# A fast product for the first FFN too: seven half products from inner block 4 on, and the modulation rows moved around it

## The chip, the core and the metric

The kernel runs on one core of one Trainium2 chip. TensorE (PE) multiplies, VectorE (DVE) and ScalarE (ACT) evaluate and prepare, GpSimd (POOL) helps, SyncE (SP) issues the loads. The metric is device microseconds of one execution. A profiled execution is one further run with the trace taken.

## The reference

Two layers of a diffusion backbone for 128 context tokens and 512 latents (640 columns), width 1024. Layer 0 mixes by pooling and short convolution, layer 1 by attention; each layer then has a SwiGLU FFN with 2816 inner columns:

```python
def modulate(x, g, shift, scale):
    return rms_norm(x, g) * (1 + scale) + shift
def swiglu(h, w_in, w_out):
    a, b = jnp.split(h @ w_in, 2, axis=-1)
    return (jax.nn.silu(a) * b) @ w_out
...
sh1, sc1, g1, sh2, sc2, g2 = ada_params(cond, w_ada[l], b_ada[l])   # silu(cond) @ w_ada[l] + b_ada[l]
x = x + g1 * mixer(modulate(x, norm_g[l, 0], sh1, sc1))
x = x + g2 * swiglu(modulate(x, norm_g[l, 1], sh2, sc2), w_ffn_in[l], w_ffn_out[l])
```

Context and latents have a condition each, so each modulation vector exists twice. All is float32.

## The kernel before

Everything is kept transposed: a tile has 128 features on the partitions and the 640 tokens in its columns, in two PSUM banks of 320. Each operand of a product is a pair, a rounded high part and the low rest (`pair`, L142 on ACT, L143 on DVE), and a product is three matmuls (high x high, high x low, low x high). `Stream` (`ws`) loads the weights in tiles of 1 MB on SP (three raw tiles), splits them into pairs, one step ahead for whole blocks and about three for half products, and `project` (matmuls L287) multiplies one output block per step; `Pipe` runs the evaluation of a block behind its matmuls. There are three PSUM tiles of two banks for products and two of one bank for small things (`ps_small`).

An FFN (`ffn`) cuts its 22 inner blocks in three groups of 8, 8 and 6. Per group the first product (`fi`) makes the blocks a and b, silu(a) * b goes as a pair into `hid`, and the second product (`fo`) adds to the residual (L500). A plain inner block costs 2 x 48 matmuls. In the layers of `FAST`, here only the second layer, the blocks from `PLAIN` = 4 on run in `fast_blocks` (L624): the block is cut in two halves of inputs, of outputs and of columns, and Winograd's seven half products take the place of eight: 7 x 12 = 84 matmuls. Their operands (`Ops.make`) are sums of halves of the normalised input, made by `operand_in` during the plain steps 1 to 4; the weights' sums are made on DVE in the raw tile (`weight`, L234 to L240) ahead of their split. The operands lie in one of the two big buffers (`bufA`, `bufB`) and two further tiles, and `hid` takes the place of the FFN's input.

The modulation vectors are rows of `w_ada` times silu of the two conditions. Most of them are computed on DVE by `AdaDve`: a row is 128 outputs, loaded as 512 KB (`rawa`), and four `tensor_tensor_reduce` (L365), for two conditions and two halves of the inputs, with the products written to a scratch tile `junk` in SBUF. `ada.run(n)` puts n rows at its place in the program, `keep_in_program_order` holds them near it; the tile framework's scheduler orders the other instructions of an engine by its own model, and on the chip every engine goes through its list in order. Of the 84 rows, 30 are done by the end of the mixer; in the first FFN one row goes with each step of `fi` and `fo` until the rest is done, which is in group 2's first product. Six raw buffers let the loads run ahead.

Of the kernel before, what the change touches and what calls it, by code (L numbers as in the profile page):

```python
# [9 lines left out]
F32 = mybir.dt.float32  # L10
F32R = mybir.dt.float32r
AF = mybir.ActivationFunctionType
# [3 lines left out]
P = 128  # L16
D = 1024
KB = D // P
# [3 lines left out]
HT = T // 2  # L22
# [7 lines left out]
WC = 256  # L30
GROUPS = ((0, 8), (8, 16), (16, 22))

FAST = (1,)
PLAIN = 4
RAW = 3
WINDOWS = (2, 4, 8, 16)
PAD = 8
UL = PAD + CTX + PAD + LAT + PAD
# [20 lines left out]
def hybrid_step(  # L59
# [22 lines left out]
    nc = tc.nc  # L82
# [16 lines left out]
    def ps_small(name):  # L99
        return psum.tile([P, 512], F32, tag="one", bufs=2, name=name)  # L100
# [45 lines left out]
    class Pipe:  # L146


        def __init__(self):
            self.due, self.now = [], 0  # L150
# [186 lines left out]
    class AdaDve:  # L337


        def __init__(self, jobs):  # L340
            self.todo = [(l, b0, n, b) for l, b0, n in jobs for b in range(n)]
            self.at, self.raw = 0, []

        def load(self):
            at = self.at + len(self.raw)
            if at < len(self.todo):
                raw = p1.tile([P, D], F32, tag="araw", bufs=6, name=f"rawa_{at}")
                nc.sync.dma_start(raw, wada[at])
                self.raw.append(raw)

        def run(self, rows, hold=True):
            for _ in range(rows):
                if self.at == len(self.todo):
                    return
                l, b0, n, b = self.todo[self.at]
                if not self.raw:
                    self.load()
                raw = self.raw.pop(0)
                self.at += 1
                if b == 0:  # L360
                    self.got = p1.tile([P, 8, 2, 2], F32, tag="got", bufs=2, name=f"got_{l}_{b0}")
                for c in range(2):
                    for q in range(2):
                        cols = slice(512 * q, 512 * q + 512)
                        op = V.tensor_tensor_reduce(  # L365
                            out=junk,
                            in0=raw[:, cols],
                            in1=silb[:, c, cols],
                            scale=1.0,
                            scalar=0.0,  # L370
                            op0=ALU.mult,
                            op1=ALU.add,
                            accum_out=self.got[:, b, c, q : q + 1],
                        )
# [289 lines left out]

            pipe.step(lambda: product(wt, p, to, fresh), after)

    def ffn(l, xin, hid, each=None, last=None, spare=None):


        def part_a(j, psa):  # L670
# [34 lines left out]
        for gi, (f0, f1) in enumerate(GROUPS):  # L705
# [12 lines left out]
                    operand_in(i - 1)  # L718

            def plain_keep(n, p):  # L720
                if held:
                    j = min(held)
                    keep(j, held.pop(j))

            if plain:
                project(f"fi{l}_{gi}", xin, KB, 2 * plain, in_done, ext=True, each=each)
# [10 lines left out]
    nc.sync.dma_start(sm, small)  # L737
    with tc.tile_pool(name="pool1", bufs=1) as p1:
        silb = p1.tile([P, 2, D], F32, tag="silb", name="silb")
        junk = p1.tile([P, 512], F32, tag="junk", name="junk")  # L740
        ada_raw = []

        def ada_load(ch):
            for q in range(4):
                raw = p1.tile([P, 2, 512], F32, tag="araw", bufs=6, name=f"raw_ada{ch}_{q}")
# [5 lines left out]
        ada = AdaDve(  # L751
            [(0, 4, 4)] + [(0, 8 * p, 8) for p in (2, 4, 3, 5)] + [(1, 8 * p, 8) for p in (1, 0, 2, 4, 3, 5)]
        )
        ada_load(2)
        nc.sync.dma_start(kc, konst)
        nc.sync.dma_start(x[:, 0:4, :], xT[:, 0:4, :])
# [8 lines left out]
        ws.load(2, cut=True)  # L765
        ada.load()
        ada.load()
        pwr = p1.tile([P, 512], F32, tag="pwr", name="pwr").rearrange("p (g c) -> p g c", g=4)
        nc.sync.dma_start(pwr, pw)
        ws.load(3)  # L770
        zero = p1.tile([P, 512], F32, tag="junk", name="zero")
        G.memset(zero, 0.0)
        zeror2 = p1.tile([P, 512], F32R, tag="zero", name="zeror")
        V.tensor_copy(zeror2, zero)
        zeror = zeror2[:, 0:P]
        G.memset(ones, 1.0 / D)
# [253 lines left out]
        assert ada.at == len(ada.todo)  # L1030


    with tc.tile_pool(name="pool2", bufs=1) as p2:
# [527 lines left out]
```

## Time and profile before

| what | us |
|---|---|
| median of 3 runs | 1395.49 (1394.67 to 1396.0) |
| the profiled execution, its own time | 1394.27 |
| its span, first to last instruction | 1392.5 |
| PE busy | 1355.6 |
| DVE busy | 1000.9 |
| ACT busy | 571.7 |

The busy share of an engine is a mean over the span; what a change in one stage is worth is read in that stage. The chain that ended last is followed back from the last instruction; a piece of it that belongs to PE is time in which nothing but PE's own work set the pace. Matmuls of the profile overlap, so their mean duration is about twice the time at which they follow one another.

### The profile page before, as it was taken

The page shows a single profiled execution, that of the slowest core. Times are in us where ns is not written, and L with a number is a line of the kernel's source. Part 1 is how long each engine was busy: PE and PEld are TensorE (multiplying, and loading weights), DVE is VectorE, ACT ScalarE, POOL GpSimd, SP SyncE. Part 2 cuts the span into 40 slices and gives each one's busy share as a digit, 9 for nine tenths or more (in the row PEclk, how much of TensorE's full clock was granted, in tenths as well). Part 3 has the DMA queues.
Part 4 walks back from the last instruction along what each step waited for, and adds up shares of the span by engine and source line. Part 5 has one row for each costly group of instructions (what it writes and reads, how often), then busy time and mean ns, then how long its engine had stood idle before and what let it go on. Part 6 is the DMA issues. An engine that isn't in the chain of part 4 may idle for free.

```text
span 1392.5 us, 22551 instructions
## 1 busy us (share of the span) xinstructions
PE 1355.6 (97%) x9139; PEld 1329.9 (96%) x9139; DVE 1000.9 (72%) x1998; ACT 571.7 (41%) x1013; POOL 69.9 (5%) x73
## 2 busy tenths in 40 slices
PE   6989999999999999999999999999999999999995
PEld 3889999999999999999999999999999999999995
DVE  4899989878777877754767677678873577536745
ACT  3433244322122221223566676557651254314543
POOL 3200000000000000000003121000000000000012
PEclk7999999999999999999999999999999999999998
DMA  9734445444434343212223111002122112311212
GB/s 365 257 120 171 177 141 176 160 143 140 164 137 166 127 169 133 100 64 72 103 75 94 47 46 39 31 31 92 61 94 88 61 62 91 121 61 61 76 46 76
DMA packets 36728, 154.50 MB, mean 111 GB/s; under 512 B 3984, under 2 KB 11152, under 8 KB 26000
## 3 DMA queue, kind: packets, MB, share of 16 engines
q1 hardware_dynamic: 36624, 153.07, 31.5%
q8 instruction: 71, 1.16, 0.3%
q14 instruction: 33, 0.27, 0.1%
HBM read 147.55 MB, written 2.88 MB: 108 GB/s over the span
## 4 chain that ended last, share of the span: by engine, by line
PE 90%; DVE 7%; issue 1%; ACT 1%; DMA 1%; SPq 0%; POOL 0%; DVEq 0%; POOLq 0%; ACTq 0%
PE fi L287 27%; PE fo L287 22%; PE fi L624 16%; PE pq L287 5%; PE pi L287 5%; PE po L287 4%; PE wb L287 2%; PE wa L287 2%; DVE junk L365 2%; PE o L1295 2%; PE s L1245 1%; PE t L1278 1%; DMA raw_ada<-wada 1%; PE fo L1430 1%; DVE x L1415 1%
## 5 line engine op out<-in xcount | busy, mean ns | idle before, releaser
L365 DVE CUSTOM_DVE_ANT_0 junk<-rawa,silb 128x512 f32<-128x512 f32 x336 | 236.6, 704 | 6.6 <-ACT silb L807 1.0
L287 PE MATMUL fi<-ah,wh_fi 128*128 128x320 f32 x832 | 191.6, 312 | 0.0
L287 PE MATMUL fi<-al,wh_fi 128*128 128x320 f32 x832 | 191.3, 311 | 0.0
L287 PE MATMUL fi<-ah,wl_fi 128*128 128x320 f32 x832 | 191.2, 311 | 0.0
L500 DVE SCALAR_TENSOR_TENSOR x<-fo,mod,x 128x128 f32<-128x128 f32 (+1 forms) x144 | 54.7, 434 | 131.2 <-PE fo L287 128.2
L287 PEld LDWEIGHTS fi<-al,wh_fi 128*128 128x128 f32 x832 | 141.0, 189 | 0.0
L287 PEld LDWEIGHTS fi<-ah,wh_fi 128*128 128x128 f32 x832 | 141.0, 190 | 0.0
L287 PEld LDWEIGHTS fi<-ah,wl_fi 128*128 128x128 f32 x832 | 140.7, 189 | 0.0
L142 ACT ACTIVATE wh_fi<-raw_fi 128x1024 fp32r<-128x1024 f32 x52 | 55.1, 1060 | 184.8 <-PE fi L287 135.9
L142 ACT ACTIVATE wh_fi_p<-raw_fi 128x512 fp32r<-128x512 f32 x126 | 77.3, 627 | 112.3 <-PE fi L624 64.9
L142 ACT ACTIVATE wh_fo<-raw_fo 128x1024 fp32r<-128x1024 f32 (+1 forms) x48 | 47.5, 990 | 180.5 <-PE fo L287 132.6
L143 DVE TENSOR_TENSOR wl_fi_p<-raw_fi,wh_fi_p 128x512 fp32r<-128x512 f32 x126 | 85.7, 689 | 48.3 <-ACT wh_fi_p L142 48.3
L624 PE MATMUL fi<-bh,wl_fi_p 128*128 128x320 f32 x288 | 88.9, 309 | 0.0
L624 PE MATMUL fi<-bh,wh_fi_p 128*128 128x320 f32 x288 | 88.9, 309 | 0.0
L624 PE MATMUL fi<-bl,wh_fi_p 128*128 128x320 f32 x288 | 88.4, 307 | 0.0
L287 PE MATMUL fo<-bh,wh_fo 128*128 128x320 f32 x352 | 80.6, 310 | 0.0
L287 PE MATMUL fo<-bh,wl_fo 128*128 128x320 f32 x352 | 80.5, 310 | 0.0
L287 PE MATMUL fo<-bl,wh_fo 128*128 128x320 f32 x352 | 80.4, 310 | 0.0
L287 PE MATMUL fo<-al,wh_fo 128*128 128x320 f32 x328 | 75.1, 310 | 0.0
L287 PE MATMUL fo<-ah,wh_fo 128*128 128x320 f32 x328 | 74.9, 309 | 0.0
L287 PE MATMUL fo<-ah,wl_fo 128*128 128x320 f32 x328 | 74.8, 309 | 0.0
L624 PE MATMUL fi<-xh,wh_fi_p 128*128 128x320 f32 x216 | 67.8, 319 | 0.1
(341 smaller groups left out, 3200.7 us busy)
## 6 DMA issues: line engine op xcount, KB each, us to landing
raw_fi<-wfi SPq DMA_DIRECT2D x44, 1024.0 KB, 4.8
rawa<-wada SPq DMA_DIRECT2D x84, 512.0 KB, 3.5
raw_fo<-wfo SPq DMA_DIRECT2D x16, 1024.0 KB, 5.0
raw_ada<-wada SPq DMA_DIRECT2D x12, 512.0 KB, 9.3
raw_in<-win SPq DMA_DIRECT2D x6, 1024.0 KB, 7.0
raw_fo<-wfo SPq DMA_DIRECT2D x8, 768.0 KB, 4.2
raw_qkv<-wqkv SPq DMA_DIRECT2D x6, 1024.0 KB, 4.8
raw_out<-wout SPq DMA_DIRECT2D x4, 1024.0 KB, 4.8
```

Source lines behind the costliest of these rows:

```text
L142: S.activation(h, src, AF.Copy)
L143: eng.tensor_tensor(out=l, in0=src, in1=h.bitcast(F32), op=ALU.subtract)
L287: PE.matmul(ps[:, h, 0 : hi - lo], w[a][:, k, cols], rhs[b][:, k0 + k, lo:hi], start=k == 0 and a == b, stop=k == kn - 1 and a == 1,)
L365: op = V.tensor_tensor_reduce(out=junk, in0=raw[:, cols], in1=silb[:, c, cols], scale=1.0, scalar=0.0, op0=ALU.mult, op1=ALU.add, accum_ou ...
L500: V.scalar_tensor_tensor(out=xs, in0=got[:, 0 : b - a], scalar=mod[l][:, gate0 + m, c : c + 1], in1=xs, op0=ALU.mult, op1=ALU.add,)
L624: PE.matmul(out, w[a][:, k, :], ops.get(OPERAND[p], b)[:, k, :], start=fresh and k == 0 and a == b, stop=k == ops.kn - 1 and a == 1, skip_ ...
L1245: PE.matmul(self.ps[:, hf, 0:HT], bufB[a][:, self.h, q0 : q0 + P], kt[b][:, self.kv, hf * HT : hf * HT + HT], start=n == 0, stop=n == 2,)
L1278: PE.transpose(flat(pt)[:, s * P : s * P + P], self.pe[:, s * P : s * P + P], ident)
L1295: PE.matmul(po[:, 0 : 2 * P], vt[a][:, self.kv, s * P : s * P + P], got[b][:, s, :], start=s == 0 and n == 0, stop=s == 4 and n == 2,)
L1415: (G if k % 3 == 1 else V).tensor_tensor(out=xs, in0=xs, in1=rstd[:, cols], op=ALU.mult)
L1430: PE.matmul(ps[m][:, h, 0 : hi - lo], w[m][a][:, k, :], bufA[b][:, k, cols], start=k == 0 and a == b, stop=k == kn - 1 and a == 1,)
```

## The change

`FAST` takes in the first layer: its inner blocks 4 to 21 run in `fast_blocks`. Its operands lie in `bufB` and two new tiles, `hid` is now `bufA`, the FFN's last product prepares the next layer's input in `bufB`, and the two names are swapped behind it. To make room, the first part's small tiles (raw rows, `junk`, `pwr`, `zero`) move to a pool that is closed after the mixer; from there on rows have two raw buffers (`bufs` 2), loaded anew from row 30 on, and `junk` is a small PSUM tile. The 46 rows of the first FFN are spread anew: one in each of the last three plain steps of group 0, one per fast block in group 0 and one per two fast blocks in groups 1 and 2 (at product 6), one and two by turns in the steps of the second product, one in each step of the last. The last eight rows (the second layer's second gate) move to the second FFN: two per fast block of group 0 (at products 1 and 6), with a new copy of silu of the conditions and scratch in PSUM.

```diff
-FAST = (1,)
+FAST = (0, 1)
+EARLY = 30
...
+        def home(self, own, rest, bufs, junk, silb):
+            self.own, self.rest, self.bufs, self.junk, self.silb = own, rest, bufs, junk, silb
...
-            if at < len(self.todo):
-                raw = p1.tile([P, D], F32, tag="araw", bufs=6, name=f"rawa_{at}")
-                nc.sync.dma_start(raw, wada[at])
+            if at < self.limit:
+                raw = self.own.tile([P, D], F32, tag="araw", bufs=self.bufs, name=f"rawa_{self.first + at}")
+                nc.sync.dma_start(raw, wada[self.first + at])
...
-                            out=junk,
+                            out=self.junk,
...
             def plain_keep(n, p):
+                if fast_each:
+                    fast_each(gi, n, p)
...
-            [(0, 4, 4)] + [(0, 8 * p, 8) for p in (2, 4, 3, 5)] + [(1, 8 * p, 8) for p in (1, 0, 2, 4, 3, 5)]
+            [(0, 4, 4)] + [(0, 8 * p, 8) for p in (2, 4, 3, 5)] + [(1, 8 * p, 8) for p in (1, 0, 2, 4, 3)]
...
+        assert ada.at == EARLY and not ada.raw
+        early.close()
+
         def last0(kn):
-            project("fo0_2", bufB, kn, KB, updater(0, 40, Norm("b0"), (bufA, 1, 0)), each=lambda i: ada.run(1))
-
-        ffn(0, bufA, bufB, each=lambda i: ada.run(1), last=last0)
+            project("fo0_2", bufA, kn, KB, updater(0, 40, Norm("b0"), (bufB, 1, 0)), each=lambda i: ada.run(1))
+
+        with tc.tile_pool(name="pool4", bufs=1) as p4:
+            ada.home(p4, p1, 2, ps_small("junk"), silb)
+            ada.limit = len(ada.todo)
+            ada.load()
+            ada.load()
+            more = tuple(p4.tile([P, 3 * 4 * HT], F32R, tag=t, name=t) for t in ("x0h", "x0l"))
+            ffn(
+                0,
+                bufA,
+                bufA,
+                each=lambda i, plain=False: ada.run(int(i >= 5) if plain else 1 + i % 2),
+                fast_each=lambda gi, n, p: ada.run(int(p == 6 and (gi == 0 or n % 2))),
+                last=last0,
+                spare=(tuple(t.rearrange("p a b -> p (a b)") for t in bufB), more),
+            )
+    bufA, bufB = bufB, bufA
...
-    ffn(1, bufA, bufA, last=last1, spare=(whole_b, more))
+    silb = p3.tile([P, 2, D], F32, tag="silb", name="silb1")
+    nc.sync.dma_start(silb, crows[None].broadcast_to((P, 2, D)))
+    S.activation(silb, silb, AF.Silu)
+    gates = AdaDve([(1, 40, 8)], 76)
+    gates.home(p3, p3, 2, ps_small("junk1"), silb)
+    ffn(
+        1,
+        bufA,
+        bufA,
+        last=last1,
+        spare=(whole_b, more),
+        fast_each=lambda gi, n, p: gates.run(int(gi == 0 and p in (1, 6))),
+    )
```

## Rows read from the trace of the kernel before

**Rows 1.** The page: busy time of each engine over the span.

```profile
PE 1355.6 (97%) x9139; PEld 1329.9 (96%) x9139; DVE 1000.9 (72%) x1998; ACT 571.7 (41%) x1013; POOL 69.9 (5%) x73
```

**Rows 2.** The chain that ended last, in order of time, over the first FFN (start us, length us, engine, tile, line, matmuls).

```profile
222.27 7.15 PE fi L287 x48
...
337.02 56.64 PE fo L287 x384
393.66 114.14 PE fi L287 x768
507.80 56.64 PE fo L287 x384
564.44 85.61 PE fi L287 x576
650.04 42.41 PE fo L287 x288
```

**Rows 3.** The same chain over the second FFN, whose inner blocks 4 to 21 already run in seven half products (the pieces between are left out).

```profile
935.80 7.14 PE fi L287 x48
...
1044.05 56.54 PE fo L287 x384
...
1201.42 56.54 PE fo L287 x384
1257.96 1.46 PE fi L624 x10
...
1333.62 32.00 PE fo L287 x216
```

**Rows 4.** Busy time by stretch over the second FFN: four plain blocks, four fast blocks, eight fast blocks (columns: stretch, length, busy PE, PEld, DVE, ACT, POOL with instructions, granted clock, DMA share, GB/s).

```profile
935.80:993.80 58.00, 58.00 (x393) 58.00 (x392) 53.65 (x88) 43.47 (x77) 0.00 (x0) 1.00 0.22 73
993.80:1044.00 50.20, 50.17 (x337) 48.98 (x337) 36.54 (x56) 26.09 (x52) 0.00 (x0) 1.00 0.26 86
...
1100.90:1201.40 100.50, 100.43 (x673) 98.11 (x673) 72.90 (x114) 51.86 (x102) 0.00 (x0) 1.00 0.24 85
```

**Rows 5.** The same view, the last 22 us of the second FFN's plain blocks.

```profile
972.00:993.80 21.80, 21.80 (x149) 21.80 (x148) 21.12 (x36) 16.23 (x30) 0.00 (x0) 1.00 0.15 50
```

**Rows 6.** The same view: the mixer's input product, the first FFN's second product of group 0, and that of group 2.

```profile
108.00:165.60 57.60, 57.60 (x389) 57.60 (x388) 56.80 (x131) 18.26 (x30) 0.33 (x6) 1.00 0.52 185
337.00:393.70 56.70, 56.70 (x387) 56.70 (x386) 41.49 (x100) 9.49 (x11) 0.00 (x0) 1.00 0.42 146
650.00:692.50 42.50, 42.50 (x291) 42.50 (x290) 29.42 (x56) 19.69 (x32) 0.00 (x0) 1.00 0.25 84
```

**Rows 7.** DVE in order of time in the first FFN's second product of group 0 (start us, us, line, operation, [idle before]): the first two of four partial sums of a modulation row, and what ends the step.

```profile
346.32 0.68 DVE L365 CUSTOM_DVE_ANT_0 junk<-rawa,silb 128x512 f32<-128x512 f32 x1
...
347.05 0.69 DVE L365 CUSTOM_DVE_ANT_0 junk<-rawa,silb 128x512 f32<-128x512 f32 x1
...
351.22 1.14 DVE L500 SCALAR_TENSOR_TENSOR x<-fo,mod,x 128x128 f32<-128x128 f32 x3 [2.01 <-PE fo L287]
```

**Rows 8.** DVE in order of time in the first FFN's second product of group 2: one step.

```profile
671.29 1.13 DVE L500 SCALAR_TENSOR_TENSOR x<-fo,mod,x 128x128 f32<-128x128 f32 x3 [1.64 <-PE fo L287]
672.34 0.34 DVE L479 SCALAR_TENSOR_TENSOR al<-x,sc,ah 128x128 fp32r<-128x128 f32 x1
672.60 0.95 DVE L143 TENSOR_TENSOR wl_fo<-raw_fo,wh_fo 128x768 fp32r<-128x768 f32 x1
673.47 0.82 DVE L422 TENSOR_TENSOR ssq_b<-ssq_b,sq_b 128x640 f32<-128x640 f32 x1
674.21 0.75 DVE L479 SCALAR_TENSOR_TENSOR al<-x,sc,ah 128x512 fp32r<-128x512 f32 x1
```

**Rows 9.** DVE in order of time at the seam from plain to fast blocks in the second FFN.

```profile
988.90 0.81 DVE L143 TENSOR_TENSOR al<-ea,ah 128x640 fp32r<-128x640 f32 x1
...
991.70 0.69 DVE L236 TENSOR_TENSOR raw_fi<-raw_fi 128x512 f32<-128x512 f32 x1
992.31 0.82 DVE L143 TENSOR_TENSOR al<-ea,ah 128x640 fp32r<-128x640 f32 x1
993.09 0.69 DVE L143 TENSOR_TENSOR wl_fi_p<-raw_fi,wh_fi_p 128x512 fp32r<-128x512 f32 x1
993.70 0.82 DVE L515 TENSOR_TENSOR eb<-fi,rstd 128x640 f32<-128x640 f32 x1
```

**Rows 10.** Groups of DVE instructions by line and shape: a difference whose second source is in PSUM (L651), in the second FFN's eight fast blocks.

```profile
L651 DVE TENSOR_TENSOR uv<-fi,uv 128x320 f32<-128x320 f32 x7 | 3.4, 488 | 1.6 <-PE fi L624 1.6
```

**Rows 11.** The same view over the first FFN's blocks of group 0: one with both sources in SBUF (L470), and a residual from PSUM (L500).

```profile
L470 DVE TENSOR_TENSOR rstd<-y_a,ssq_a 128x320 f32<-128x320 f32 x2 | 0.9, 490 | 0.0
...
L500 DVE SCALAR_TENSOR_TENSOR x<-po,mod,x 128x320 f32<-128x320 f32 x1 | 0.5, 544 | 0.0
```

**Rows 12.** ACT in order of time at the second FFN's start: a load of its function table and the instruction behind it.

```profile
949.20 1.28 ACT L673 ACT_TABLE_LOAD   x1
950.50 1.02 ACT L673 ACTIVATE ea<-ea 128x128 f32<-128x128 f32 x2
```

**Rows 13.** The start's SiLU of the conditioning rows (duration ns min/median/max).

```profile
L807 ACT ACTIVATE silb<-silb x1: 1892/1892/1892, 33.6 to 33.6; 128x2048 f32<-128x2048 f32 x1
```

**Rows 14.** Who SP's DMA queue waited for over the first FFN (us in total, times, longest us).

```profile
SPq L220 <- DVE wl_fi L143: 104.4, 22, 13.9
```

**Rows 15.** DMA issues over the same stretch (count, KB each, median us from issue to landing).

```profile
rawa<-wada SPq DMA_DIRECT2D x49, 512.0 KB, 3.4
```

More of the change, by code (lines that the diff above doesn't have):

```diff
@@ L337, in hybrid_step, with __init__ @@
     class AdaDve:
-        def __init__(self, jobs):
+        def __init__(self, jobs, first=0):
             self.todo = [(l, b0, n, b) for l, b0, n in jobs for b in range(n)]
-            self.at, self.raw = 0, []
+            self.at, self.raw, self.first = 0, [], first
+            self.limit = len(self.todo)
+        def home(self, own, rest, bufs, junk, silb):
+            self.own, self.rest, self.bufs, self.junk, self.silb = own, rest, bufs, junk, silb
         def load(self):
             at = self.at + len(self.raw)
-            if at < len(self.todo):
-                raw = p1.tile([P, D], F32, tag="araw", bufs=6, name=f"rawa_{at}")
-                nc.sync.dma_start(raw, wada[at])
+            if at < self.limit:
+                raw = self.own.tile([P, D], F32, tag="araw", bufs=self.bufs, name=f"rawa_{self.first + at}")
+                nc.sync.dma_start(raw, wada[self.first + at])
                 self.raw.append(raw)
@@ L360, in run @@
                 if b == 0:
-                    self.got = p1.tile([P, 8, 2, 2], F32, tag="got", bufs=2, name=f"got_{l}_{b0}")
+                    self.got = self.rest.tile([P, 8, 2, 2], F32, tag="got", bufs=2, name=f"got_{l}_{b0}")
                 for c in range(2):
@@ L365, in run @@
                         op = V.tensor_tensor_reduce(
-                            out=junk,
+                            out=self.junk,
                             in0=raw[:, cols],
-                            in1=silb[:, c, cols],
+                            in1=self.silb[:, c, cols],
                             scale=1.0,
@@ L665, in fast_blocks, with ffn @@
             pipe.step(lambda: product(wt, p, to, fresh), after)
-    def ffn(l, xin, hid, each=None, last=None, spare=None):
+    def ffn(l, xin, hid, each=None, last=None, spare=None, fast_each=None):
         def part_a(j, psa):
@@ L725, in ffn @@
             if plain:
-                project(f"fi{l}_{gi}", xin, KB, 2 * plain, in_done, ext=True, each=each)
+                project(f"fi{l}_{gi}", xin, KB, 2 * plain, in_done, ext=True, each=each and (lambda i: each(i, True)))
             if l in FAST:
@@ L739, in hybrid_step @@
         silb = p1.tile([P, 2, D], F32, tag="silb", name="silb")
-        junk = p1.tile([P, 512], F32, tag="junk", name="junk")
+        early = ExitStack()
+        p0 = early.enter_context(tc.tile_pool(name="pool0", bufs=1))
+        junk = p0.tile([P, 512], F32, tag="junk", name="junk")
         ada_raw = []
@@ L744, in ada_load @@
             for q in range(4):
-                raw = p1.tile([P, 2, 512], F32, tag="araw", bufs=6, name=f"raw_ada{ch}_{q}")
+                raw = p0.tile([P, 2, 512], F32, tag="araw", bufs=6, name=f"raw_ada{ch}_{q}")
                 nc.sync.dma_start(raw, wada0[(ch + 1) // 2 if ch < 3 else 2, q])
@@ L751, in hybrid_step @@
         ada = AdaDve(
-            [(0, 4, 4)] + [(0, 8 * p, 8) for p in (2, 4, 3, 5)] + [(1, 8 * p, 8) for p in (1, 0, 2, 4, 3, 5)]
+            [(0, 4, 4)] + [(0, 8 * p, 8) for p in (2, 4, 3, 5)] + [(1, 8 * p, 8) for p in (1, 0, 2, 4, 3)]
         )
+        ada.home(p0, p1, 6, junk, silb)
+        ada.limit = EARLY
         ada_load(2)
@@ L767, in hybrid_step @@
         ada.load()
-        pwr = p1.tile([P, 512], F32, tag="pwr", name="pwr").rearrange("p (g c) -> p g c", g=4)
+        pwr = p0.tile([P, 512], F32, tag="pwr", name="pwr").rearrange("p (g c) -> p g c", g=4)
         nc.sync.dma_start(pwr, pw)
         ws.load(3)
-        zero = p1.tile([P, 512], F32, tag="junk", name="zero")
+        zero = p0.tile([P, 512], F32, tag="junk", name="zero")
         G.memset(zero, 0.0)
-        zeror2 = p1.tile([P, 512], F32R, tag="zero", name="zeror")
+        zeror2 = p0.tile([P, 512], F32R, tag="zero", name="zeror")
         V.tensor_copy(zeror2, zero)
@@ L1447, in hybrid_step @@
     more = tuple(p3.tile([P, 3 * 4 * HT], F32R, tag=t, name=t) for t in ("xh", "xl"))
-    ffn(1, bufA, bufA, last=last1, spare=(whole_b, more))
+    silb = p3.tile([P, 2, D], F32, tag="silb", name="silb1")
[11 more added lines that the diff above has]
+    )
+    assert gates.at == 8
 def _constants():
```

2 lines of the change are left out of this document (1 added, 1 removed).

## Prediction

> **What bounds the kernel now.** I read the page first: TensorE (PE) is busy 97% of the span, VectorE (DVE) 72%, ScalarE (ACT) 41% [rows 1]. Then the chain of waits over both FFNs: there it is one run of PE pieces with hardly a gap [rows 2, 3], so a matmul removed there is time removed, as long as nothing else becomes late. The reader should lay the two chains side by side: the second FFN already does what the change brings to the first, and so prices it. Third, the busy time by stretch: DVE is nearly full in the second FFN's plain blocks (53.65 of 58.00 us) and 73% busy in its fast blocks [rows 4]; in the mixer's input product it is busy 56.80 of 57.60 us and PE still never waits [rows 6]. So DVE is close behind PE, and whatever is added to it must be counted stage by stage.
>
> **What the change removes.** Fast against plain, taken as stages. First FFN: group 0 runs from 222.27 to 337.02 (114.75), group 1 114.14, group 2 85.61 [rows 2], together 314.5. Second FFN: 935.80 to 1044.05 (108.25), then from the end of its second product (1044.05 + 56.54 = 1100.59) to 1201.42 (100.83), then 1257.96 to 1333.62 (75.66) [rows 3], together 284.74. The difference is 29.8 us, all of it PE time on the chain. The second products have the same shape in both (56.64 and 56.54) and stay.
>
> **What it adds to DVE.** The fast blocks of the first FFN get the second FFN's DVE work, and the modulation rows come on top. One row is four partial sums; two in a row start 0.73 us apart (346.32, 347.05) [rows 7], so a row costs 2.9 us. By count of the calls, 46 rows now lie in the first FFN: 3 in the last three plain steps, 4 in group 0's fast blocks, 12 in each of the first two second products (one and two by turns), 4 in group 1, 3 in group 2, 8 in the third second product, which had none. Eight more lie in the second FFN's four fast blocks of group 0. I take the places in order.
>
> *First FFN, seam to group 0's fast blocks.* The second FFN shows the same stretch without rows. From 972.0 to 993.8 DVE idles 0.68 us [rows 5]. Three rows are 8.7 us. Of the work done there, three differences of kept blocks (0.74 each, between 988.90 and 992.31), one weight difference and one split (0.6 each) aren't due yet and can go behind [rows 9]: 3.4. So the evacuation of the last plain block, now at 993.70 [rows 9], comes 8.7 - 0.7 - 3.4 = 4.6 us late, and a fast product needs its PSUM bank. One product can run before that one, 12.57 / 7 = 1.8 us (100.50 us for eight blocks [rows 4]). PE loses about 3. After that four rows (11.6) meet 50.20 - 36.54 = 13.7 us of DVE idle [rows 4]: covered.
>
> *First and second of the second products.* A step has 2.01 us of DVE idle with one row in it [rows 7]; with one and two by turns, two steps have 2 x 2.01 - 2.9 = 1.1 us left. Covered on average; what DVE is late with at the end falls on the next group's first weights. *Groups 1 and 2*: idle of 100.50 - 72.90 = 27.6 us in eight blocks [rows 4] against four rows, 11.6. For all of these together 1 us.
>
> *Third second product.* A step of DVE is 5.30 us less 1.64 of idle, 3.66 [rows 8]; with a row 6.56, against PE's 42.41 / 8 = 5.30 [rows 2]. DVE computes the weights' low parts one step ahead, so PE may trail by one step. The first DVE step, which starts some 2.2 us into the product (an estimate: the last block's keep, as at the end of the second FFN's groups), ends at 8.8; its seventh starts at 8.8 + 5 x 6.56 = 41.6, gives block 7's weights 0.9 later, at 42.5, where PE wants them at 7 x 5.30 = 37.1: 5.4 us lost. The rows stand in DVE's queue ahead of the residual and of the norm's operand, so the qkv product's first block is late by little more; it reads that operand's last part at its end.
>
> *Second FFN, group 0.* Eight rows, 23.2 us, meet 13.7 us of idle: 9.5 over. At 993.8 four products have their weights (the fourth split is at 993.09 [rows 9]); three of them beyond the running one are 5.4 us of PE work, less the 1.2 us that a difference and a split take: 4.1 of slack. PE loses 5.4; the rest of the lag runs off in the second product behind, which carries no rows.
>
> *Second FFN, start.* A SiLU over 2048 columns took 1.89 us [rows 13], and it now stands on ACT's queue between the logarithm's table and the norm's chain: up to two table loads of 1.30 (949.20 to 950.50) [rows 12], so 0 to 4.5 us before the norm's sums, for which PE waits there. Behind it queue the squares and the scaled operands. ACT has gaps earlier, so I take 1. The scratch of the sums now holds one of two small PSUM tiles through each FFN, so that the norm's second half may wait for the first; other PE work can go ahead of it: 0.5. Together 1.5.
>
> [...]
>
> *Scratch in PSUM.* No DVE write to PSUM is in the trace. A read costs nothing by one row (488 against 490 ns for 320 columns), 54 ns by another (544) [rows 10, 11], and another reason against a gain is not to be had, so 0 to 0.22 us a row either way; I take 0, since the 490 and 488 are the same operation. Over the 19 rows where DVE is short that is up to 4.2 us.
>
> [...]
>
> *Moved loads.* A row's load now has two buffers instead of six. It is issued when the row two before is read, and lands after 3.4 us [rows 15]; a row (2.9) and half a step usually lie between, so I cost it at nothing; without this cover see the fourth case. The load of the rotary tables waits on SP for memory that the last row frees, later than before; behind it queue later qkv weights, which have three tiles in hand. The first FFN's operand tiles take over memory freed at the end of the mixer; first use is at the second plain block. Nothing for either.
>
> **The sum.** 29.8 - 3 - 1 - 5.4 - 5.4 - 1.5 = 13.5 us. The profiled execution took 1394.27 (span 1392.5, 1.8 us around it), so its like after is 1380.8; against the median of 1395.49, 1.2 above it, 1382.0.
>
> **The rivals.** *Second case: DVE's load is hidden.* For it: the mixer's input product at 99% DVE without a PE wait [rows 6]; the sums may be spread into gaps and the lag carried into light stretches. Only the third second product is over by arithmetic in every order: 29.8 - 5.4 = 24.4, 1371.1.
>
> *Third case, slower than before: the rows hold up the weights.* In a fast block DVE makes differences and splits for every 1.8 us product, ACT's copies wait for the differences, and PE's releases wait for ACT, all in order. A row put ahead delays all three. 19 rows of 2.9 lie in fast blocks (11 and 8): 55 us. With 5.4 and 1.5 for the other places, the change turns into a loss where more than (29.8 - 6.9) / 55 = 42% of their time reaches PE. At 60% it is 33 - 22.9 = 10 slower, 1405.6. For it: in-order queues and the eight rows that are over. Against it: 27% idle in the fast blocks.
>
> *Fourth case: rows starve.* SP stood up to 13.9 us at one weight load [rows 14], with row loads behind it. Two steps of the second products have 1.1 us to spare, 8.8 over eight pairs of steps; if each of the 24 rows there waited 0.93 us, the 13.5 of the sum would be gone: 1395.5. Against it: the load waits and the weight waits are both freed by DVE, in its own order.
>
> **How the numbers follow.** Chances: forecast 0.57 (own range 1374 to 1389), second 0.22 (1364 to 1374), third 0.13 (1389 to 1415), fourth 0.08 (1389 to 1400). The bounds of the unknown costs (4.2 for PSUM, 3 more for the table, the two losses of 5.4 by half either way) make the forecast's range. A measurement can tell some 0.2%, 2.8 us, from no change. Faster: forecast, second, and 0.05 of the last two, 0.84; within: 0.04; slower: 0.12. The range for 8 in 10 is 1368 to 1396.
>
> **What would show it.** Right: fi stages of the first FFN near the second's lengths, PE gaps at the seam to group 0, in the third second product (some 48 us instead of 42.4, DVE near full) and in the second FFN's first fast blocks (55 to 56 instead of 50.2). Sums at 690 ns show PSUM free. Wrong: PE waits in groups 1 and 2, DVE waiting for row loads, or no gaps in the three places.

## The result and the profile after

The changed kernel takes 1377.47 us, median of four runs (1376.99 to 1378.86), against 1395.08 (1394.53 to 1396.0) for the kernel before beside them: a ratio of 0.9877 [0.9865, 0.9888], 17.6 us less. The forecast was 1382.0, 13.5 less. The profiled execution is one of the four and took 1376.99; its span is 1375.2.

The page of the changed kernel, busy time of each engine (it answers to [rows 1]):

```profile
PE 1327.7 (97%) x8929; PEld 1294.1 (94%) x8929; DVE 1081.2 (79%) x2182; ACT 636.3 (46%) x1155; POOL 70.3 (5%) x73
```

PE has 27.9 us less to do and DVE 80 more. PE's 97% says nothing of where the 12 us between 29.8 and 17.6 went; for that the span is cut by stages. Busy time by stretch of the changed kernel, columns as in [rows 4]: first FFN's group 0, its second product, group 1, its second product, group 2, its second product; last line the second FFN's group 0.

```profile
222.70:337.40 114.70, 110.23 (x729) 108.44 (x728) 104.37 (x200) 68.38 (x124) 0.00 (x0) 0.99 0.32 115
337.40:393.90 56.50, 56.50 (x385) 56.50 (x385) 52.44 (x130) 9.54 (x12) 0.00 (x0) 1.00 0.49 168
393.90:495.10 101.20, 100.97 (x676) 98.51 (x675) 85.14 (x157) 51.29 (x101) 0.00 (x0) 1.00 0.34 115
495.10:552.30 57.20, 57.11 (x386) 56.84 (x385) 52.21 (x129) 9.55 (x12) 0.00 (x0) 1.00 0.49 166
552.30:630.00 77.70, 76.12 (x508) 73.91 (x507) 63.92 (x121) 37.77 (x75) 0.00 (x0) 1.00 0.30 106
630.00:672.50 42.50, 42.50 (x290) 42.50 (x289) 42.36 (x105) 20.07 (x31) 0.00 (x0) 1.00 0.50 172
...
916.40:1027.10 110.70, 108.22 (x728) 106.81 (x727) 106.36 (x208) 69.92 (x126) 0.00 (x0) 1.00 0.29 98
```

Three stretches show a PE that isn't busy all the time: the first FFN's group 0 (4.5 us idle, and a granted clock of 0.99), group 2 (1.6), the second FFN's group 0 (2.5). The sixth line is the one to look at twice: DVE is busy 42.36 of 42.50 us and PE all of it.

The same cut by PE's first matmul of each stage, for the profiled executions of all kernels of this study (us; "pattern" is the second FFN of the kernel before, which has no rows in it, from the chain of [rows 3]; "to FFN 2" runs from the qkv product's first matmul to the second FFN's first; in e7 four matmuls of the qkv product run 3 us before the end of the last `fo` and are counted in it):

| kernel | group 0 | fo | group 1 | fo | group 2 | fo | to FFN 2 | FFN 2 group 0 |
|---|---|---|---|---|---|---|---|---|
| before | 114.75 | 56.64 | 114.14 | 56.63 | 85.61 | 42.41 | 243.35 | 108.25 |
| pattern | 108.25 | | 100.83 | | 75.66 | | | |
| after | 114.65 | 56.54 | 101.19 | 57.21 | 77.69 | 42.50 | 243.92 | 110.68 |
| e1_short_all | 108.21 | 56.54 | 100.97 | 56.71 | 75.87 | 42.49 | 244.11 | 108.28 |
| e2_short_plain | 107.96 | 56.55 | 101.49 | 56.93 | 77.71 | 42.50 | 244.41 | 110.75 |
| e3_short_fast | 111.40 | 56.54 | 101.53 | 57.21 | 77.70 | 42.50 | 244.05 | 110.66 |
| e4_short_gates | 115.74 | 56.54 | 101.15 | 57.21 | 77.75 | 42.50 | 244.55 | 108.38 |
| e5_two_first | 115.83 | 56.55 | 101.10 | 56.92 | 77.00 | 42.50 | 244.52 | 110.66 |
| e6_early_rows | 109.11 | 56.54 | 101.19 | 57.21 | 77.70 | 42.50 | 244.45 | 110.67 |
| e7_rows_to_last | 114.90 | 56.54 | 101.20 | 57.20 | 77.48 | 49.57 | 243.63 | 110.68 |
| e8_gates_spread | 114.82 | 56.54 | 101.21 | 57.20 | 77.70 | 42.50 | 244.16 | 109.59 |
| e9_spread | 109.12 | 56.54 | 101.13 | 57.21 | 76.77 | 42.50 | 244.42 | 109.61 |
| e10_all_first | 109.11 | 56.54 | 101.12 | 57.22 | 77.09 | 42.49 | 244.02 | 108.07 |

Against the pattern the changed kernel loses 6.4 in group 0 (it comes out no shorter than it was before), 0.9 in group 1 with the second product behind it, 2.0 in group 2, 0.1 in the last second product, 0.6 on the way to the second FFN, 2.4 in that one's group 0: 12.4 together, where 17.3 us between the two profiled executions (1394.27 and 1376.99) leave 12.5 of the 29.8.

**The seam.** PE in order of time in the changed kernel, where the first FFN's first fast block begins (start us, us, line, [idle before <- releaser]):

```profile
288.41 0.41 PE L630 MATMUL fi<-bh,wh_fi_p 128*128 128x320 f32 x1 [0.22 <-ACT sa L648]
...
289.52 0.42 PE L630 MATMUL fi<-bh,wl_fi_p 128*128 128x320 f32 x1 [0.55 <-DVE wl_fi_p L145]
...
292.25 0.31 PE L630 MATMUL fi<-bl,wh_fi_p 128*128 128x320 f32 x1
292.40 0.31 PE L630 MATMUL fi<-bh,wl_fi_p 128*128 128x320 f32 x1
296.35 0.61 PE L630 MATMUL fi<-x0h,wh_fi_p 128*128 128x320 f32 x1 [3.64 <-DVE uv L652]
296.75 0.47 PE L630 MATMUL fi<-x0l,wh_fi_p 128*128 128x320 f32 x1
297.02 0.47 PE L630 MATMUL fi<-x0h,wl_fi_p 128*128 128x320 f32 x1
```

One wait of 3.64 us, ended by L652: the addition with which DVE reads a half product from the PSUM tile that the next product writes to. Behind the wait matmuls follow at 0.27 us (296.75, 297.02) instead of 0.15 (292.25, 292.40). DVE in order of time, same kernel, same place (all its 2182 instructions stand in the trace in the order of the program's list, as the 1998 of the kernel before do):

```profile
281.10 0.82 DVE L521 TENSOR_TENSOR eb<-fi,rstd 128x640 f32<-128x640 f32 x1
...
284.26 0.69 DVE L371 CUSTOM_DVE_ANT_0 junk<-rawa,silb 128x512 f32<-128x512 f32 x1
284.87 0.14 DVE L371 DVE_READ_ACCUMULATOR2_ANT got<- 128x1 f32 x1
284.87 0.82 DVE L145 TENSOR_TENSOR al<-ea,ah 128x640 fp32r<-128x640 f32 x1
285.61 0.69 DVE L371 CUSTOM_DVE_ANT_0 junk<-rawa,silb 128x512 f32<-128x512 f32 x1
...
293.90 0.69 DVE L371 CUSTOM_DVE_ANT_0 junk<-rawa,silb 128x512 f32<-128x512 f32 x1
...
294.51 0.69 DVE L145 TENSOR_TENSOR wl_fi_p<-raw_fi,wh_fi_p 128x512 fp32r<-128x512 f32 x1
...
295.72 0.48 DVE L652 TENSOR_TENSOR uv<-fi,uv 128x320 f32<-128x320 f32 x1
```

Two things are to be seen. The evacuation of the last plain block's second half (L521, 281.10) stands right behind that block's last matmul: it isn't late, as the forecast had it. The rows' sums have gone behind it, in turns with the kept blocks' differences, and eight of them (284.26 to 293.90) stand ahead of L652. They hold up more than L652: by the order of the splits, the last split ahead of it (L145, 294.51 to 295.20) makes the waiting product's weights. These came 1.0 us before L652 ended, so without L652 most of the 3.64 would still have been a wait, for the weights.

### The profile page after: what moved, and what is told of

Its sections match the earlier page's. It is cut to its first block, busy times and chain, and to the rows that moved or that the text cites. A ratio compares the mean times of both kernels' runs of the same rounds, so it can differ in the third digit from the quotient of the medians.

```text
span 1375.2 us, 22538 instructions
## 1 busy us (share of the span) xinstructions
PE 1327.7 (97%) x8929; PEld 1294.1 (94%) x8929; DVE 1081.2 (79%) x2182; ACT 636.3 (46%) x1155; POOL 70.3 (5%) x73
## 4 chain that ended last, share of the span: by engine, by line
PE 77%; DVE 16%; ACT 3%; issue 2%; DMA 1%; SPq 0%; POOL 0%; DVEq 0%; ACTq 0%; POOLq 0%
PE fi L630 24%; PE fo L289 21%; PE fi L289 7%; PE pq L289 5%; PE pi L289 5%; DVE junk L371 5%; PE po L289 4%; DVE wl_fi_p L145 3%; PE wb L289 2%; PE wa L289 2%; PE o L1326 2%; PE s L1276 1%; PE t L1309 1%; ACT wh_fi_p L144 1%; DMA raw_ada<-wada 1%
## 5 line engine op out<-in xcount | busy, mean ns | idle before, releaser
L144 ACT ACTIVATE wh_fi_p<-raw_fi 128x512 fp32r<-128x512 f32 x252 | 153.9, 626 | 219.5 <-PE fi L630 108.6
L145 DVE TENSOR_TENSOR wl_fi_p<-raw_fi,wh_fi_p 128x512 fp32r<-128x512 f32 x252 | 170.1, 686 | 64.1 <-ACT wh_fi_p L144 63.9
L630 PE MATMUL fi<-ah,wl_fi_p 128*128 128x320 f32 x288 | 88.8, 308 | 0.0
L630 PE MATMUL fi<-al,wh_fi_p 128*128 128x320 f32 x288 | 88.7, 308 | 0.0
L630 PE MATMUL fi<-ah,wh_fi_p 128*128 128x320 f32 x288 | 88.4, 307 | 0.0
L289 PE MATMUL fo<-al,wh_fo 128*128 128x320 f32 x352 | 80.8, 310 | 0.0
L630 PE MATMUL fi<-x0h,wh_fi_p 128*128 128x320 f32 x216 | 69.0, 323 | 5.0 <-DVE uv L652 3.6
L630 PE MATMUL fi<-x0l,wh_fi_p 128*128 128x320 f32 x216 | 66.9, 311 | 0.0
L630 PE MATMUL fi<-x0h,wl_fi_p 128*128 128x320 f32 x216 | 66.9, 311 | 0.0
L289 PE MATMUL pi<-ah,wh_in 128*128 128x320 f32 (+1 forms) x256 | 62.3, 326 | 4.7 <-ACT ev L526 3.8
```

The source lines that it names most:

```text
L144: S.activation(h, src, AF.Copy)
L145: eng.tensor_tensor(out=l, in0=src, in1=h.bitcast(F32), op=ALU.subtract)
L289: PE.matmul(ps[:, h, 0 : hi - lo], w[a][:, k, cols], rhs[b][:, k0 + k, lo:hi], start=k == 0 and a == b, stop=k == kn - 1 and a == 1,)
L630: PE.matmul(out, w[a][:, k, :], ops.get(OPERAND[p], b)[:, k, :], start=fresh and k == 0 and a == b, stop=k == ops.kn - 1 and a == 1, skip_ ...
```

## The experiments

**Theory A**: the whole missing 12.2 us are DVE's time for the rows, most of it in three places (seam, second FFN's group 0, seam to group 2). **Rival B**: a part of it is something else that the change brought (scratch in PSUM, two raw buffers, SiLU and its table, the memory handed on), and stays when the rows cost nothing. Four kernels shorten the sums of chosen rows from 512 to 16 columns and keep all else; a sum of 16 columns still takes 181 ns in the mean, one of 512 takes 695:

```diff
-                        cols = slice(512 * q, 512 * q + 512)
+                        cols = slice(512 * q, 512 * q + (16 if CHOSEN else 512))
...
-                            out=self.junk,
+                            out=self.junk[:, 0 : cols.stop - cols.start],
```

with `row = self.first + self.at - 1` chosen as `row >= 30` (e1), 30 to 32, the rows of the plain steps (e2), 33 to 36, those of group 0's fast blocks (e3), and `row >= 76`, the eight of the second FFN (e4).

> The changed kernel with every modulation row from row 30 on (46 in the first FFN, 8 in the second) cut to 16 of 512 columns in each of its four sums; loads, instructions and places stay, 31 of 32 parts of the sums are left out. Of the 29.8 us that the seven products take off TensorE, 17.6 came through; 12.2 went elsewhere. Theory A, the forecast's: the missing 12.2 us are VectorE time of the rows; then this gives 1395.1 - 29.8 = 1365.3, between 1364 and 1367.5. Rival B: they belong to what else the change brings (scratch in PSUM, two buffers for the rows, SiLU and the norm at the second FFN's start, the fast blocks' own weights); then the time stays above 1373.

Measured: 1365.57, ratio 0.9789 [0.9774, 0.9803], 29.4 us under the 1394.94 of the kernel before beside it. In the table every stage is within 0.3 us of the pattern but the way to the second FFN. B falls but for the scratch in PSUM: without the rows' time the change gives the 29.8 almost in full. Of the scratch e1 says little, since most of the writing to it went with the columns; the durations of the sums, further down, say more.

> The changed kernel with only rows 30 to 32, those of the last three plain steps of the first FFN, cut to 16 of 512 columns. The stage from 222.9 to 337.5 us is 6.4 us longer than its like in the second FFN. The forecast's step (these three rows delay the evacuation of the last plain block): all but 1 of the 6.4 comes back, 1371.5 to 1372.5, and cutting the four rows of the fast blocks instead brings 1 at most. Rival, the sum of work: VectorE is over its time in the whole stage, whichever row is cut, and its lag shows later, in the fast blocks: three rows are 7.4 us, so this brings 5 to 6.4 too, but so does the other cut.

> The changed kernel with only rows 33 to 36, one in each of the first FFN's four fast blocks of group 0, cut to 16 of 512 columns. The forecast's step: no more than 1 us, 1376.5 or above. Sum of work: four rows are 9.8 us, more than the stage is over; 6.4 us come back, 1371 to 1372.

Measured: e2 1371.10, ratio 0.9829 [0.9815, 0.9844]; e3 1374.30, ratio 0.9851 [0.9837, 0.9866]. The three plain rows bring 6.4 when they go, the four fast rows 3.2. So the loss at the seam is not the plain rows' alone: with the fast rows gone, the plain ones still cost 3.2; together they cost twice that, and the fast rows, alone, nothing. PE's wait and the DVE operation that ends it, of e3 and of e2:

```profile
294.36 0.38 PE L630 MATMUL fi<-x0h,wh_fi_p 128*128 128x320 f32 x1 [1.57 <-DVE uv L652]
```

```profile
289.69 0.69 DVE L238 TENSOR_TENSOR raw_fi<-raw_fi 128x512 f32<-128x512 f32 x1
290.30 0.49 DVE L652 TENSOR_TENSOR uv<-fi,uv 128x320 f32<-128x320 f32 x1
```

In e2 L652 starts at 290.30, 5.4 earlier than after the change, and PE has no wait there; the four full sums of the first fast row (283.97 to 287.88) stand shortly ahead of it all the same. In e3 the wait is 1.57. Of the 3.2 us by which the fast rows make group 0 longer when the plain ones are there (111.40 against 114.65), 1.8 are PE's waits (2.66 against 4.47 in all) and 1.4 are matmuls at the lower clock (PE busy 108.74 against 110.18; over 295 to 300 us the granted clock was 1.00 in e3 and 0.66 after the change).

> The changed kernel with only the eight rows of the second FFN cut to 16 of 512 columns. If the rows are what makes that FFN's group 0 longer (110.7 against 108.3 us before), 2.4 us come back: 1375.0, between 1374.3 and 1375.8. If the SiLU, its load or the PSUM tile held through the FFN cost it, the time stays at 1377.0 or above.

Measured: 1375.74, ratio 0.9861 [0.9845, 0.9878], 1.7 less. The second FFN's group 0 is 108.38: 2.3 of its 2.4 are back. The profiled execution, 1376.71, is the slowest of the four (the others 1375.42 to 1375.82): in it group 0 of the first FFN took 115.74, though nothing was changed there. The clock goes with that: after the same wait (3.6 us) it stayed low for longer. Stretches of 5 us from 290 (295 for e4), columns as above (the granted clock is the third figure from the end); first the changed kernel, then e4:

```profile
290.00:295.00 5.00, 2.71 (x19) 2.44 (x17) 5.00 (x13) 1.91 (x4) 0.00 (x0) 1.00 0.29 98
295.00:300.00 5.00, 3.65 (x16) 3.69 (x17) 5.00 (x10) 1.94 (x4) 0.00 (x0) 0.66 0.47 136
300.00:305.00 5.00, 5.00 (x35) 4.81 (x34) 4.87 (x13) 2.06 (x5) 0.00 (x0) 1.00 0.43 179
```

```profile
295.00:300.00 5.00, 3.69 (x14) 3.72 (x15) 5.00 (x10) 1.97 (x4) 0.00 (x0) 0.50 0.51 134
300.00:305.00 5.00, 5.00 (x30) 4.81 (x29) 4.42 (x11) 1.40 (x3) 0.00 (x0) 0.84 0.43 180
```

Next, the rows' places, one at a time.

> The changed kernel with the turns of the second products swapped: two rows in even steps and one in odd ones, so that the last step before groups 1 and 2 has one row instead of two. Group 2's blocks are 1.8 us longer than with short rows, with a TensorE wait for the last residual (0.48 us) and one for ScalarE's copy behind it (0.95 us). If four sums less between the last residual and the group's start are what these wait for: 1 to 1.5 us come back, 1376 to 1376.5. If the lag comes from the three rows inside group 2: no change, 1377.5.

```diff
-                each=lambda i, plain=False: ada.run(int(i >= 5) if plain else 1 + i % 2),
+                each=lambda i, plain=False: ada.run(int(i >= 5) if plain else 2 - i % 2),
```

Measured: 1377.72, ratio 0.9871 [0.9856, 0.9886]: no difference. By stages, 0.7 came back in group 2 and 0.3 in the product ahead of it, and 1.2 went in group 0, with the clock again (115.83 in this profile; granted 0.50 over 295 to 300 us and 0.83 over 300 to 305). That two rows in the last step delay the next group is thus shown by the stage only, not by the time. The stage shows it twice, however: with three rows inside group 2 it goes from 77.69 to 77.00 (e5), with none inside from 77.48 (e7) to 76.77 (e9 below). The rows inside the group cost 0.2 in either pair (e9 differs from these kernels in other places too).

> The changed kernel with the rows of the plain steps 5 to 7 of the first FFN placed at steps 0 and 1 (two rows), and the third in group 1, block 4. Theory (VectorE's sums at the seam delay the release of a PSUM tile in the first fast block, and TensorE's clock falls in that wait): the gap and the slow stretch behind it shrink, fi of group 0 goes from 114.7 to 109 to 111, the time to 1372 to 1374. Rival (the sum of VectorE work from the first plain step on decides, wherever a row stands, since it has hardly any idle time there): only the row that leaves the stage counts, 2.4 us, 1375.

```diff
-                each=lambda i, plain=False: ada.run(int(i >= 5) if plain else 1 + i % 2),
-                fast_each=lambda gi, n, p: ada.run(int(p == 6 and (gi == 0 or n % 2))),
+                each=lambda i, plain=False: ada.run(int(i < 2) if plain else 1 + i % 2),
+                fast_each=lambda gi, n, p: ada.run(int(p == 6 and (gi == 0 or n % 2 or (gi == 1 and n == 4)))),
```

Measured: 1372.02, ratio 0.9827 [0.9811, 0.9843], 5.5 us under the changed kernel. Two rows go to the first two plain steps, the third to group 1, and none stands in the last plain steps before the seam. The rival falls: two of the three rows still lie in the stage, and it is 5.5 shorter. The whole of group 0 in e6:

```profile
222.50:331.60 109.10, 108.58 (x728) 107.02 (x727) 102.77 (x192) 68.61 (x124) 0.00 (x0) 1.00 0.33 116
```

Against 222.70:337.40 of the changed kernel PE idles 0.5 instead of 4.5 and is busy 108.58 instead of 110.23: 4.0 us are the wait, 1.6 the matmuls at the lower clock (0.99 over the stage there, 1.00 here).

> The changed kernel with group 2's three rows moved into the first FFN's last second product, at its steps 1, 3 and 5, which have two rows then. The forecast's step (rows stand ahead of residuals and of the next weights, 6.56 us a step against TensorE's 5.30) charges it each row in full: 3 x 2.5 = 7.4 us more there, less 1 in group 2: 1383 to 1384. Rival (sums slip behind what is due, as the trace of the changed kernel shows, 42.5 us for that product): the lag of 7.4 us falls on the qkv product's norm, which has slack of some 9 us: 1376 to 1379.

```diff
-            project("fo0_2", bufA, kn, KB, updater(0, 40, Norm("b0"), (bufB, 1, 0)), each=lambda i: ada.run(1))
+            project("fo0_2", bufA, kn, KB, updater(0, 40, Norm("b0"), (bufB, 1, 0)), each=lambda i: ada.run(1 + int(i in (1, 3, 5))))
...
-                fast_each=lambda gi, n, p: ada.run(int(p == 6 and (gi == 0 or n % 2))),
+                fast_each=lambda gi, n, p: ada.run(int(p == 6 and (gi == 0 or n % 2 and gi < 2))),
```

Measured: 1384.05, ratio 0.9917 [0.9902, 0.9932], 6.6 slower than the changed kernel, as the forecast's step has it; the rival falls. The last second product of e7, and PE's waits in its whole profile that belong to it (us in total, times, longest):

```profile
630.00:679.60 49.60, 45.45 (x294) 44.66 (x293) 49.46 (x129) 20.28 (x31) 0.00 (x0) 0.97 0.52 179
```

```profile
PE fo L289 <- DVE wl_fo L145: 4.1, 3, 2.3
```

Three more rows, 7.07 us more: 2.4 us a row, in full. DVE is busy 49.46 of the 49.60 us and sets the length; PE shows it as 4.1 of waits, and most of the rest as matmuls that take longer (busy 45.45 against 42.50, with a granted clock of 0.97 against 1.00). With eight rows DVE stood almost at the limit (42.36 of 42.50). And the rows taken out of group 2 brought only 0.2 there.

> The changed kernel with two of the second FFN's eight rows at its plain steps 0 and 1 and six in the fast blocks (at product 6, and at product 1 of the third and fourth). The eight rows cost 2.3 us there. If VectorE's idle time at the FFN's start (some 3 us before the norm's scale is there) takes two rows: 1.5 to 2 come back, 1375.5 to 1376. If they only push the operands later: no change, 1377.5, or up to 1 slower.

```diff
+        each=lambda i, plain=False: gates.run(int(plain and i < 2)),
...
-        fast_each=lambda gi, n, p: gates.run(int(gi == 0 and p in (1, 6))),
+        fast_each=lambda gi, n, p: gates.run(int(gi == 0 and (p == 6 or p == 1 and n > 1))),
```

Measured: 1376.56, ratio 0.9863 [0.9848, 0.9878]; the stage gives 1.1 back of its 2.4, the time 0.9, between the two forecasts. (The kernel before took 1394.94, 1395.74 and 1395.50 beside the three series of runs, so a difference below 1 us between times of different series says little without the stage.) Six rows still lie in the four fast blocks.

> All moves together, from the rule that a row costs nothing where VectorE has the time in that stage and its whole 2.45 us where it has not: rows at plain steps 0 and 1, one in each fast block of groups 0 and 1 and none in group 2 (8 x 2.45 = 19.6 us against 27.6 us of idle in group 1), two rows in even and one in odd steps of the second products, and the second FFN's rows as two at its plain steps 0 and 1 and six in the fast blocks. If the stages add up: 1372.0 - 1.8 (group 2) - 0.3 - 1.1 (second FFN) = 1368.8, between 1368 and 1370. If each TensorE wait is set by the place of single sums and not by the stage's sum, the eight rows of group 1 open new waits: 1371 or above.

```diff
-                each=lambda i, plain=False: ada.run(int(i >= 5) if plain else 1 + i % 2),
-                fast_each=lambda gi, n, p: ada.run(int(p == 6 and (gi == 0 or n % 2))),
+                each=lambda i, plain=False: ada.run(int(i < 2) if plain else 2 - i % 2),
+                fast_each=lambda gi, n, p: ada.run(int(p == 6 and gi < 2)),
```

and the edit of e8.

> The changed kernel with all 54 rows in the first FFN, none in the second, and so without its SiLU, its load and its scratch: two at plain steps 0 and 1, one in every fast block (18), 13 in each of the first two second products, 8 in the last. By the stages' sums every place still fits (group 1 19.6 us of 27.6 idle, group 2 14.7 of some 20, a second product 13 x 2.45 = 31.9 and 17 of its own in 56.6): the second FFN gives back 2.3, group 2 keeps its 1.8, 1372.0 - 2.3 = 1369.7, between 1368.5 and 1371. If VectorE's lag at the last second product's start, which has no time to spare, grows with group 2's rows, each row too many costs 2.4 there: 1374 or above.

```diff
-            [(0, 4, 4)] + [(0, 8 * p, 8) for p in (2, 4, 3, 5)] + [(1, 8 * p, 8) for p in (1, 0, 2, 4, 3)]
+            [(0, 4, 4)] + [(0, 8 * p, 8) for p in (2, 4, 3, 5)] + [(1, 8 * p, 8) for p in (1, 0, 2, 4, 3, 5)]
...
-                each=lambda i, plain=False: ada.run(int(i >= 5) if plain else 1 + i % 2),
-                fast_each=lambda gi, n, p: ada.run(int(p == 6 and (gi == 0 or n % 2))),
+                each=lambda i, plain=False: ada.run(int(i < 2) if plain else 1 + int(i in (0, 1, 2, 4, 6))),
+                fast_each=lambda gi, n, p: ada.run(int(p == 6)),
...
-    silb = p3.tile([P, 2, D], F32, tag="silb", name="silb1")
-    nc.sync.dma_start(silb, crows[None].broadcast_to((P, 2, D)))
-    S.activation(silb, silb, AF.Silu)
-    gates = AdaDve([(1, 40, 8)], 76)
-    gates.home(p3, p3, 2, ps_small("junk1"), silb)
...
-        fast_each=lambda gi, n, p: gates.run(int(gi == 0 and p in (1, 6))),
```

Measured: e9 1370.20 (1369.69 to 1370.66), ratio 0.9819 [0.9805, 0.9832]; e10 1368.69 (1367.7 to 1371.34), ratio 0.9811 [0.9798, 0.9825]. Both beat both kernels; which of the two is faster the times don't decide. e10 is inside its range. e9 missed its range (1368 to 1370) by a little, and not for the rival's reason: the eight rows opened no wait in group 1 (101.13). The 1.8 hoped for in group 2 came back by half only (77.69 to 76.77), though none of its rows is left there: PE's 0.95 us wait for ACT's copy (L642) stays, and only in e1 it is gone. In e10 all 54 rows lie in the first FFN, the second is without them, and the two stretches that tell are these (first FFN's second product of group 0, then group 2):

```profile
331.00:388.00 57.00, 57.00 (x389) 57.00 (x389) 55.90 (x142) 9.53 (x11) 0.00 (x0) 1.00 0.52 185
546.00:622.00 76.00, 74.90 (x500) 72.83 (x500) 68.91 (x139) 37.35 (x74) 0.00 (x0) 1.00 0.35 122
```

Thirteen rows instead of twelve fill DVE to 98% of the second product and cost PE nothing there. The largest piece that is left of the row time in e10 is 1.4 us at group 2, 77.09 against the pattern's 75.66, of which that wait for ACT's copy, behind DVE's last residual, is 0.95; group 0 keeps 0.9 and the product ahead of group 2 0.6.

## Why the prediction was right, and where its terms were off

The time lay inside the forecast's own range (1374 to 1389), 4.5 us under its value. The gain and the kind of loss were the forecast's: DVE late at a few places. The places were right in part, and that the sum came so near is in part luck: two terms were too small by 5.3 together, three too big by 9.8. Of the forecast's own signs the gaps at the seam and in the second FFN came (2.4 us there instead of 5.4); the one in the third second product did not, and a sign of being wrong, a PE wait in group 2, did (1.4 us).

- **The gain, 29.8.** Right: with the rows' time taken away the kernel is 29.4 faster (e1).
- **Seam and group 0, 3.** It measured 6.4. Two steps failed. By the first, the evacuation of the last plain block comes 4.6 us late and a fast product needs its PSUM bank: that evacuation is on time, and what is late is L652, a release among the half products themselves, with the weights just ahead of it, at the second fast block's second product. By the second, the four rows of the fast blocks are covered by 13.7 us of DVE idle there. They would be, by the sum, but the idle time lies behind the wait. The first of the four rows comes while DVE still carries the lag of the plain ones, and so adds to the wait (e2 against e3: 3.2 for the plain rows alone, as forecast, and 3.2 more with the fast ones). A quarter of the loss, 1.6, is the lower clock behind the wait (0.66 over 295 to 300 us), for which the forecast had no term.
- **Second products and groups 1 and 2, 1.** It measured 2.9, 2.0 of it at group 2, where the last step of the product before has two rows and the next product needs the residual's PSUM tile and ACT's copies. The forecast put it with "the next group's first weights"; the profile shows waits for the residual (0.48) and for ACT (0.95) instead. That it hangs on the order of one and two rows shows in the stages only (e5, and e9 against e7), where that order is worth 0.7; the wait for ACT stays when the order is turned and is gone in e1 alone.
- **Third second product, 5.4.** It measured 0.1, the largest miss. The step of 6.56 us for DVE against 5.30 for PE was wrong in two places, seen in one step of DVE after the change (order of time; it answers to [rows 8]):

```profile
645.42 0.95 DVE L145 TENSOR_TENSOR wl_fo<-raw_fo,wh_fo 128x768 fp32r<-128x768 f32 x1
646.29 0.69 DVE L371 CUSTOM_DVE_ANT_0 junk<-rawa,silb 128x512 f32<-128x512 f32 x1
646.90 0.14 DVE L371 DVE_READ_ACCUMULATOR2_ANT got<- 128x1 f32 x1
646.90 1.12 DVE L506 SCALAR_TENSOR_TENSOR x<-fo,mod,x 128x128 f32<-128x128 f32 x3
...
648.21 0.69 DVE L371 CUSTOM_DVE_ANT_0 junk<-rawa,silb 128x512 f32<-128x512 f32 x1
...
650.24 0.69 DVE L371 CUSTOM_DVE_ANT_0 junk<-rawa,silb 128x512 f32<-128x512 f32 x1
650.85 0.14 DVE L371 DVE_READ_ACCUMULATOR2_ANT got<- 128x1 f32 x1
650.85 0.95 DVE L145 TENSOR_TENSOR wl_fo<-raw_fo,wh_fo 128x768 fp32r<-128x768 f32 x1
```

A sum with other work behind it takes 0.61 of DVE (646.29 to 646.90, 650.24 to 650.85), not the 0.73 of two in a row: a row is 2.4, as e7 confirms. And only three sums lie in this step, 5.43 us from one split to the next: rows don't stay with their steps. By the grouped lines of the stretch 630.0 to 672.6, 27 of the 32 sums ran in it and six of the eight splits; two splits had been made before and the sums at the end ran beside the next product. So the capacity is that of the whole product and its edges, not of one step; counted so, it is just enough. The rule behind the step, that what DVE can't hold is lost in full, is what e7 shows from the ninth row on (7.07 us for three rows of 2.4).
- **Second FFN's group 0, 5.4.** It measured 2.4, all of it the eight rows (e4). The forecast's overhang of 9.5, at 2.4 a row instead of 2.9, is 8 x 2.4 - 13.7 = 5.5; less its slack of 4.1, that is 1.4. The size of a row takes 4.0 off the term, which was 3.0 too big; the 1.0 between 1.4 and 2.4 I did not take apart.
- **Second FFN's start, 1.5.** It measured 0: SiLU ran inside the product before, one table load came with it where the forecast allowed for two, and PE has no wait at the FFN's start. In the chain the next long piece begins 1.33 us behind the FFN's first 48 matmuls (923.71 to 925.04), before the change 1.34. ACT in order of time, after:

```profile
901.50 1.28 ACT L1481 ACT_TABLE_LOAD   x1
902.80 1.92 ACT L1481 ACTIVATE silb<-silb 128x2048 f32<-128x2048 f32 x1
```

  The instruction behind the load starts 1.30 after it, as in [rows 12].

- **Scratch in PSUM, 0.** Right: a sum became some 5 ns longer. Groups of the stretch from the first FFN's start to the end of its last product, where all products go to PSUM after the change and to SBUF before it (first the changed kernel, then the kernel before):

```profile
L371 DVE CUSTOM_DVE_ANT_0 junk<-rawa,silb 128x512 f32<-128x512 f32 x180 | 125.1, 695 | 4.7 <-DMA rawa<-wada 2.2
L371 DVE DVE_READ_ACCUMULATOR2_ANT got<- 128x1 f32 x180 | 25.2, 140 | 0.0
```

```profile
L365 DVE CUSTOM_DVE_ANT_0 junk<-rawa,silb 128x512 f32<-128x512 f32 x215 | 148.3, 690 | 4.8
L365 DVE DVE_READ_ACCUMULATOR2_ANT got<- 128x1 f32 x215 | 17.8, 83 | 0.0
```

  A sum takes 695 ns against 690, and the reading of the accumulator behind it 140 against 83. The 0.06 of the reading shows where two sums follow each other (0.79 from start to start against 0.73), and not where other work lies between (0.61 in both kernels). The two rows that the forecast compared ([rows 10, 11]) are an addition and a multiplication, both TENSOR_TENSOR, not the same operation; no run here tells whether that matters.

- **The rivals.** The second (DVE's load hidden but for the third product, 1371.1) named the wrong exception: that product is hidden, the seam is not. The third (rows hold up the weights, from 42% of their time on) had the mechanism at the seam, where L652 and the weights ahead of it are late, but of all 54 rows, some 54 x 2.4 = 130 us, PE lost 12, a tenth. The fourth falls: DVE waited 2.2 us for row loads in all (the line above), and e1 shows that it cost nothing.

Left open: the 0.6 us between the first FFN and the second, which stays in e1 (0.8 there, 244.11 against 243.35; from 0.3 in e7 to 1.2 in e4) and so isn't the rows' time, and stays in e10 (0.7), which has no SiLU, row load or scratch in the second FFN, and so isn't theirs either; and whether scratch in SBUF would change anything, which wasn't tried.

## What to carry to other kernels

Cover was a matter of place here, not of sums: the four rows of group 0's fast blocks, 2.4 us each, cost 3.2 behind those of the plain steps, although the pattern has 13.7 us of DVE idle in these blocks, because that idle time lies behind the wait. The three rows ahead of the seam gave back 5.5 when they were moved (e6) and 6.4 when they were shortened (e2). So put added work behind a seam or well ahead of it, not right before it. Count an engine's capacity over a whole stage and its two edges, since work slipped over step boundaries (27 of the last second product's 32 sums ran in it); past that capacity 7.2 us of added rows lost 7.07 (e7). And price an added instruction by the spacing it has between other work (0.61 here), not by that of two of its kind in a row (0.73).

## What the hardware showed that was not expected

- Behind the PE wait of 3.64 us that ended at 296.35 in the changed kernel the granted clock was 0.50 over 296 to 299 us, 0.91 over 299 to 300 and 1.00 over 300 to 305 (matmuls at 0.27 us instead of 0.15); with a wait of 1.57 us in the same place (e3) it was 1.00 from 290 to 305 us. In e7's last second product, with three waits of 4.1 us in all, the longest 2.3, it was 0.97 over 630.0 to 679.6. How long it stayed low differed between executions with the same wait of 3.6: over 295 to 300 and 300 to 305 us it was 0.66 and 1.00 after the change, 0.50 and 0.84 in e4, which goes with 1.1 us of time (114.65 against 115.74 for group 0). A difference of 1 us between two of these profiles can be this alone.
- In the kernel before, the next DVE instruction started 0.61 us after an accumulating sum if it was another kind of operation (225.72, 226.33) and 0.73 if it was a sum of the same kind (346.32, 347.05); with the sums' products written to PSUM the latter is 0.79 (550.28, 551.07, 551.86 in the changed kernel), the former still 0.61 (646.29, 646.90). The difference of 0.06 is that of the accumulator's reading, 140 against 83 ns.
